# Layer 1's experts as whole fp32 products on column tiles, over 96 or 64 tokens each

## The chip, the cores and the metric

One core of a Trainium2 chip runs the whole program. The metric is device time in microseconds (us), the median of the runs of a kernel. The core has five engines that work side by side: TensorE (PE: matmuls; PEld: its weight loads), VectorE (DVE), ScalarE (ACT), GpSimd (POOL) and SyncE (SP), which issues the large loads from HBM. A matmul takes a stationary operand of up to 128 rows by 128 columns and streams a moving operand of up to 512 columns past it into PSUM, which has 8 banks of 128 rows by 512 fp32 columns.

## The reference

Four layers over 256 tokens of width 1024: two of a first block (a mixed attention layer with a dense feed-forward, then a convolution layer with eight experts), two of a second block (each with cross attention and sixteen small experts). The change is in the eight experts of the first block's second layer, "layer 1":

```
logits = tokens @ router_w                    # 256 tokens, 8 experts
top_vals, top_idx = top_k(logits, 2)          # two experts per token
gates = softmax(top_vals)
y[expert e, its tokens] = (silu(x @ w1[e]) * (x @ w3[e])) @ w2[e]      # 1024 -> 2816 -> 1024, fp32
out[token] = sum over its two experts of gate * y
```

The weights of one expert are three matrices of 1024 x 2816 fp32, 33 MB (of 1,048,576 bytes); eight experts take 264 MB. On the reference's inputs its router sends 79, 56, 13, 76, 83, 72, 64 and 69 tokens to experts 0 to 7.

## The kernel before

**Loads.** All weights come through `raw` (line 193): the next slot of a ring of 8 KB-per-partition slots is taken, and SP issues one load of 1 MB into it. SP works through its loads in program order; a load waits until the last reader of its slot is done. In the experts of layer 1 the ring has 8 slots. Five more slots (`WH1`) belong to `wsplit`.

**fp32 accuracy from fp32r.** `wsplit` (line 243) turns each half of a load into a high part (ScalarE, line 254, a copy to fp32r) and a low part (VectorE, line 255, the difference). `mm3` (lines 187 to 191) then makes three fp32r products: high by high, high by low, low by high.

**An expert of layer 1** (`moe`, class `Job`, line 1201 on). The tokens of an expert are gathered into 128 places by products with a one-hot matrix (line 1191), once for the high and once for the low part of x. `up` (line 1217) goes over the hidden units in blocks of 512 (the last 256): for w1, then for w3, eight 128-row steps of `mm3` with the tokens as stationary operand, then Silu on ScalarE (line 1228) or the product on VectorE (line 1230). `turn` (line 1232) transposes the block's result and splits it, `down` (line 1241) multiplies it by w2 with `mm3` into two banks that hold the expert's output; `combine` (line 1257) splits that, multiplies by the transposed one-hot matrix (line 1265) and adds to the sum with the gate (line 1269). The order in which the parts are written is up(w3) of a block, up(w1) of the next with `turn` inside it, `combine` of the expert before, `down`. A planner places instructions on the engines by its own estimate of their costs, with this order as priority, so that short pieces move between longer ones.

An expert with more than 128 tokens leads to a second pass over all experts, behind a branch (line 1311); no expert of these inputs has so many. Four loads of the next stage (`PRIME`) are issued ahead of the branch.

**The second block's experts** (`moe2`) already work without split weights: 64 gathered tokens per batch, products in fp32 with `tile_position`, that is with the 128 columns of TensorE taken as two tiles of 64, line 1654 (up) and line 1680 (down); the number of an expert can be read from memory into a register of SP (line 1702), and the address of a load follows from it. Other places use four column tiles of 32: adaLN (line 444, 512 columns), the convolution (line 1003, 256 columns), the router (line 1131).

Of the kernel before, what the change touches and what calls it, by code (L numbers as in the profile page):

```python
# [35 lines left out]
MID = 4  # L36
NSLOT, NSLOTB, WHB = 11, 2, 4
CONV = "pvpvpvpp"
PBIG = 8

# [27 lines left out]
def host_consts():  # L68
# [24 lines left out]
    # what a difference has to be above: below zero where the earlier of two equals comes first  # L93
# [61 lines left out]
class Net:  # L155
# [6 lines left out]
    # ---------------------------------------------------------------- helpers  # L162
# [60 lines left out]
    def more_raw(self, name, n):  # L223
        """n more slots for the weights as they come."""
# [6 lines left out]
    def halves(self, name, n):  # L231
        """n slots where wsplit puts its parts."""
# [4 lines left out]
    def take(self, shape, dt, name, p=None):  # L237
        """a tile in a slot of the ring (p, or the one that is free first), until it is given back."""
# [4 lines left out]
    def wsplit(self, x):  # L243
        """raw [128, a, b] -> a pairs (hi, lo) of [128, b]."""
# [14 lines left out]
    def table(self, func):  # L259
        """has ScalarE load the table of func ahead of its use."""  # L260
# [9 lines left out]
    def ordered(self):  # L270
        """a part whose instructions VectorE and ScalarE take in the order given here."""
# [3 lines left out]
    def after(self, *ins):  # L275
        """what follows queues up behind these on their engines."""
# [5 lines left out]
    def rsqrt(self, v, tile=None):  # L282
        """1 / sqrt(v) by Newton's iteration, column by column for the few columns of a tile of its own."""
# [24 lines left out]
    def rms_rstd(self, x2, n, eps, meanwhile=None):  # L308
        """x2: list of lists of APs per token tile, rstd [128, tiles]; meanwhile: what VectorE does before."""
# [19 lines left out]
    def transpose4(self, srcs, name="tp", tag="b"):  # L329
        """up to four [128,128] f32 blocks transposed into one bank."""  # L330
# [5 lines left out]
    def to_T(self, x, hi, lo, cols=slice(0, 256), scale=None, shift=None, k0=0, keep=None):  # L336
        """x: [128, 2, n*128] natural -> hi/lo[:, k0+k, cols]; optional per-feature scale and shift."""
# [21 lines left out]
    def weights_in(self, w, c0, n=512):  # L359
        """w: [1024, *] DRAM view, columns c0..c0+n by 1 MB, as raw() takes them."""  # L360
# [4 lines left out]
    def wstream(self, w, c0, n=512):  # L365
        """(hi, lo) of [128, n] for each 128 rows, in order."""
# [3 lines left out]
    def steps_T(self, w, c0, xT, ntok, evac, n=512, tag="g"):  # L370
        """out[n128, tokens] for each 128 columns; evac(i, psum[:, :ntok]). One step for each 128 rows of w."""
# [14 lines left out]
    def steps_N(self, w, c0, xT, toks, evac, n=512):  # L386
        """out[tok128, n]; evac(i, psum)."""
# [23 lines left out]
    # ---------------------------------------------------------------- setup  # L411
# [62 lines left out]
    def gate_rows(self, mrow, j0, post, dst):  # L474
        """dst[128, 1024] = gt * post_g on every partition."""
# [11 lines left out]
    def norm_T(self, x, hi, lo, cols, sc, pool, tag="raw", bufs=1, fill=0):  # L487
        """modulated rmsnorm of natural x into hi/lo."""
# [8 lines left out]
    def resid(self, y, gp, yg):  # L497
        """X += rmsnorm(y) * gp; y: per token tile two [128,512] APs; yg: room for y * gp, may be y itself."""
# [44 lines left out]
    # ---------------------------------------------------------------- memory keys and values  # L543
# [10 lines left out]
    def last_v(self):  # L554
        """the values of the last layer, from whole operands: no work for ScalarE and VectorE in it."""
# [11 lines left out]
    def fillers(self):  # L567
        """memory keys and values of both layers but for last_v, in steps for where TensorE would wait."""
# [13 lines left out]
    # ---------------------------------------------------------------- layer 0  # L582
    def layer0(self):
# [3 lines left out]
        with ExitStack() as es:  # L587
# [26 lines left out]
            # gates  # L614
# [55 lines left out]
            # lambda  # L670
# [23 lines left out]
            # mLSTM queries, keys, values  # L694
# [34 lines left out]
            # mLSTM: both directions over [x | ctx]  # L729
# [69 lines left out]
            # differential attention  # L799
# [26 lines left out]
            def gate():  # L826
                # output gate of the mLSTM
# [116 lines left out]
    # ---------------------------------------------------------------- layer 1  # L944
# [4 lines left out]
    def conv1(self, mrow):  # L949
        nc, t, tc = self.nc, self.t, self.tc  # L950
        with tc.tile_pool(name="l1", bufs=1) as lp:
# [33 lines left out]
            def conv_pe(i):  # L985
                """four taps at once: 32 channels at each of four shifts on the rows, a column tile for each 32 channels."""
# [104 lines left out]
    def moe_rows(self, mrow, sp):  # L1091
        """rows g*(1+sc) and sh of the second half of layer 1, on every partition."""
# [25 lines left out]
    def logits_in(self, u, uT, tt, copy):  # L1118
        """u [128, 2, 1024], natural, into columns tt of uT [128, KC, 256]."""
# [4 lines left out]
    def logits(self, uT, tt, rw, lt, pl, copy):  # L1124
        """the logits of token tile tt into pl [128, E] of PSUM."""
# [51 lines left out]
    def moe(self, E, F, uh, oh0, G, slot, ci, w1, w3, w2, acc, mp):  # L1177
# [23 lines left out]
        class Job:  # L1201
            """one expert over its gathered tokens, in pieces that the caller interleaves."""
            def __init__(j, w1e, w3e, w2e, oh, gcol, first):
# [6 lines left out]
                if not first:  # L1210
                    j.rest()
# [688 lines left out]
```

## Time and profile before

| | |
|---|---|
| median of 3 runs | 2331.29 us (2331.14 to 2337.98) |
| profiled execution, span from the first to the last instruction | 2325.3 us |
| TensorE / VectorE / ScalarE busy | 2196.3 / 1458.7 / 1115.3 us |
| HBM read | 631.2 MB (10^6 bytes), 272 GB/s over the span |
| share of it for layer 1's experts | 264 loads of 1024 KB |

The profile shows one execution. Busy time counts an engine's own instructions; TensorE's matmuls are pipelined and their ends are modelled, so what it can do is read from the distances between starts and not from busy time. An fp32 matmul leaves two records, an fp32r one leaves one. The idle time before an instruction is put down to what released it.

### The profile page before, as it was taken

The numbers are of one execution on the slowest core, as the hardware profiler recorded it, in microseconds if no ns is written. First come the engines' busy times: TensorE is split into PE (matmuls) and PEld (weight loads), VectorE is DVE, ScalarE is ACT, GpSimd is POOL, SyncE is SP. The second block draws the span as 40 slices with busy tenths as digits, with TensorE's granted clock in tenths as the row PEclk, the third lists the DMA queues.
The fourth block names the chain that finished last, engine by engine and source line by source line (L and its number), as shares of the span: only waits on it lengthen the run. The fifth ranks groups of instructions, "written<-read, shape, count | busy, mean of one in ns | idle before, by whom it ended". The sixth has DMA issues, their size and how long they took to land. (4 is left out here: it accounts for less than half of the span.)

```text
span 2325.3 us, 30656 instructions
## 1 busy us (share of the span) xinstructions
PE 2196.3 (94%) x11817; PEld 1560.6 (67%) x11817; DVE 1458.7 (63%) x2261; ACT 1115.3 (48%) x1530; POOL 82.1 (4%) x121
## 2 busy tenths in 40 slices
PE   6999979999899999999999999988899998999997
PEld 2776648888676888888888888867543436843442
DVE  4464575446886889889898888876622226732223
ACT  3443354335436777777777777765211113421111
POOL 1010100000300000000000000001000001000000
PEclk8999989999999999999999999999899998989998
DMA  7533567863326999999999999966699985499991
GB/s 272 199 110 134 184 228 253 270 223 132 110 92 217 337 343 351 328 344 351 337 354 337 335 335 344 340 231 225 227 392 396 377 306 184 164 365 395 391 364 37
DMA packets 283841, 634.45 MB, mean 273 GB/s; under 512 B 11696, under 2 KB 69168, under 8 KB 277536
## 3 DMA queue, kind: packets, MB, share of 16 engines
q1 hardware_dynamic: 281312, 630.75, 75.5%
q8 instruction: 99, 1.62, 0.3%
q0 software_dynamic: 2080, 1.04, 0.2%
q10 hardware_dynamic: 288, 0.52, 0.1%
q14 instruction: 62, 0.51, 0.1%
HBM read 631.20 MB, written 1.05 MB: 272 GB/s over the span
## 5 line engine op out<-in xcount | busy, mean ns | idle before, releaser
L255 DVE TENSOR_TENSOR wh<-raw,wh 128x1024 fp32r<-128x1024 f32 x710 | 851.8, 1222 | 250.2 <-ACT wh L254 243.9
L254 ACT ACTIVATE wh<-raw 128x1024 fp32r<-128x1024 f32 x710 | 740.5, 1058 | 374.2 <-PE y L191 90.9
L189 PE MATMUL up<-wh,xgh 128*128 128x512 f32 (+1 forms) x768 | 293.2, 382 | 0.0
L190 PE MATMUL up<-wh,xgh 128*128 128x512 f32 (+1 forms) x768 | 289.4, 377 | 0.0
L191 PE MATMUL up<-wh,xgl 128*128 128x512 f32 (+1 forms) x768 | 289.2, 377 | 0.0
L1654 PE MATMUL up<-raw,xg 128*64 128x512 f32 x1088 | 260.2, 596 | 0.0
L1654 PEld LDWEIGHTS up<-raw,xg 128*64 128x64 f32 x1088 | 82.7, 137 | 144.7 <-issue 139.6
L190 PE MATMUL y<-wh,hTh 128*128 128x512 f32 x440 | 173.4, 394 | 0.0
L191 PE MATMUL y<-wh,hTl 128*128 128x512 f32 x440 | 170.1, 396 | 3.4 <-DVE hTl L1238 3.4
L189 PE MATMUL y<-wh,hTh 128*128 128x512 f32 x440 | 171.3, 396 | 0.5 <-ACT hTh L1237 0.5
L191 PEld LDWEIGHTS up<-wh,xgl 128*128 128x128 f32 x768 | 144.3, 188 | 29.1 <-DVE xgl L1197 0.2
L190 PEld LDWEIGHTS up<-wh,xgh 128*128 128x128 f32 x768 | 144.4, 188 | 27.8 <-DVE wh L255 0.2
L189 PEld LDWEIGHTS up<-wh,xgh 128*128 128x128 f32 x768 | 144.3, 188 | 27.8
L1680 PE MATMUL y<-raw,hT 128*64 128x512 f32 x544 | 152.1, 597 | 0.0
L1659 DVE TENSOR_TENSOR h<-up,h 64x512 f32<-64x512 f32 x34 | 23.4, 689 | 199.6 <-ACT h L1658 199.6
L1658 ACT ACTIVATE h<-up 64x512 f32<-64x512 f32 x34 | 20.1, 592 | 198.8 <-PE up L1654 198.8
L1680 PEld LDWEIGHTS y<-raw,hT 128*64 128x64 f32 x544 | 49.1, 136 | 85.1 <-issue 81.7
L189 PE MATMUL gT<-fuTh,wh 128*128 128x256 f32 x352 | 101.0, 287 | 0.0
L190 PE MATMUL gT<-fuTl,wh 128*128 128x256 f32 x352 | 99.5, 283 | 0.0
L191 PE MATMUL gT<-fuTh,wh 128*128 128x256 f32 x352 | 99.5, 283 | 0.0
L191 PEld LDWEIGHTS y<-wh,hTl 128*128 128x128 f32 x440 | 81.9, 187 | 25.5 <-DVE hTl L1238 6.9
L189 PEld LDWEIGHTS y<-wh,hTh 128*128 128x128 f32 x440 | 82.5, 188 | 19.9 <-ACT hTh L1237 0.7
(555 smaller groups left out, 3538.8 us busy)
## 6 DMA issues: line engine op xcount, KB each, us to landing
raw<-in_l_moe_w SPq DMA_DIRECT2D x264, 1024.0 KB, 5.5
raw<-in_w_gate SPq DMA_DIRECT2D x64, 1024.0 KB, 10.5
raw<-in_w_up SPq DMA_DIRECT2D x64, 1024.0 KB, 11.0
raw<-in_w_down SPq DMA_DIRECT2D x64, 1024.0 KB, 9.1
raw<-in_l_mod_w SPq DMA_DIRECT2D x48, 1024.0 KB, 6.3
raw<-in_l_ffn_w SPq DMA_DIRECT2D x33, 1024.0 KB, 5.3
raw<-in_l_w_in SPq DMA_DIRECT2D x14, 1024.0 KB, 5.4
raw<-in_l_conv_pw_w SPq DMA_DIRECT2D x12, 1024.0 KB, 5.6
```

The lines of the kernel that those rows point to most:

```text
L189: mm(out, l[0], r[0], start=start, stop=False, skip_group_check=True)
L190: mm(out, l[0], r[1], start=False, stop=False, skip_group_check=True)
L191: mm(out, l[1], r[0], start=False, stop=stop, skip_group_check=True)
L254: nc.scalar.activation(hi, x[:, k:k + s, :], AF.Copy)
L255: nc.vector.tensor_tensor(lo, x[:, k:k + s, :], hi.bitcast(F32), OP.subtract)
L1654: nc.tensor.matmul(p[o:o + 64, :], xg[:, k, c0:c0 + 64], x[w][:, k - k4, :], start=(k == 0), stop=(k == KC - 1), tile_position=(0, o))
L1658: nc.scalar.activation(h[c0:c0 + 64], p[c0:c0 + 64, :], AF.Silu)
L1659: nc.vector.tensor_tensor(h[c0:c0 + 64], p[o:o + 64, :], h[c0:c0 + 64], OP.mult)
L1680: nc.tensor.matmul(y[o][i * 64:(i + 1) * 64, :], hT[:, q * m + i * 64:q * m + (i + 1) * 64], x[i % len(x)][:, k, o * 512:(o + 1) * 512], s ...
```

## The change

It replaces the products of layer 1's experts. No weight is split; a product is one fp32 matmul. Experts are sorted by their number of tokens (expert 0 is always first, and static, the others are read as register values by SP); the first five (`NL`) get 96 places, the other three 64. `PLACES` is the order in which they run: by places 96, 64, 96, 96, 64, 96, 96, 64. With 96 tokens the columns are four tiles of 32, and the three tiles of tokens by w1 and w3 by two halves of a block make twelve products per 128-row step in three banks; with 64 tokens two tiles of 64 and four products in two banks. Blocks have 1024 hidden units (the last 768), and a load holds two 128-row steps of 1024 columns (4 KB runs; w2: two whole rows per partition, 8 KB runs). Gathered x and the hidden units are kept in fp32; high and low part of x are summed in one bank by the gather. The five slots of `wsplit` join the ring of loads. `combine` has to add two partial results for the second half of the columns when there are 96 tokens. PSUM is divided anew for this stage: three banks for up, two for y, three for the rest. The branch to the second pass is taken when an expert has more tokens than its places. Comments are dropped in the whole file.

```
-MID = 4
+NL, PLACES = 5, (0, 5, 1, 2, 6, 3, 4, 7)
...
     def __init__(j, ws, oh, m, gcol, first):
         ...
+        for k0 in (0, 4):
+            p = self.bank("xg")
+            for i in range(4):
+                o = p[:, i * m:(i + 1) * m]
+                for q in range(4):
+                    nc.tensor.matmul(o, uh[q // 2][:, q % 2, (k0 + i) * 128:(k0 + i + 1) * 128], oh[:, q % 2, :m],
+                                     start=(q == 0), stop=(q == 3))
+            (nc.vector.tensor_copy if k0 else nc.scalar.copy)(xg[:, k0:k0 + 4, :m], ...)
...
     def up(j, i):
+        f0, n = blocks[i]
+        hn, m = n // 2, j.m
+        nb = 3 if m == 96 else 2
+        ps = [self.bank("up", "g") for _ in range(nb)]
+        if m == 96:
+            t, plan = 32, [(0, 0, 0, 0, 0), (0, 1, 0, 0, 32), (0, 2, 0, 0, 64), (0, 3, 0, 1, 64),
+                           (1, 0, 0, 1, 0), (1, 1, 0, 1, 32), (1, 2, 1, 1, 0), (1, 3, 1, 1, 32),
+                           (2, 0, 1, 0, 0), (2, 1, 1, 0, 32), (2, 2, 1, 0, 64), (2, 3, 1, 1, 64)]
+        else:
+            t, plan = 64, [(0, 0, 0, 0, 0), (0, 1, 1, 0, 0), (1, 0, 0, 1, 0), (1, 1, 1, 1, 0)]
+        for k2 in range(0, KC, 2):
+            x = [self.raw(w[:, k2:k2 + 2, f0:f0 + n], 2, n) for w in j.w]
+            for k in range(k2, k2 + 2):
+                for b, c, w, half, s in plan:
+                    nc.tensor.matmul(ps[b][c * t:(c + 1) * t, :hn], j.xg[:, k, s:s + t],
+                                     x[w][:, k - k2, half * hn:(half + 1) * hn], start=(k == 0), stop=(k == KC - 1),
+                                     tile_position=(0, c * t), skip_group_check=True)
+        (three parts of Silu on ScalarE, then three of the product on VectorE; two each with 64 tokens)
...
     def turn(j, i):
+        hv = h[:, :n].rearrange("s (p k) -> s k p", k=nk)      # columns nk apart
+        (nk transposes in groups of four, one copy to SBUF for each group)
...
     def down(j, i):
+        if m == 96:
+            t, one = 32, [(0, 0, 0, 0), (0, 1, 0, 32), (0, 2, 0, 64), (0, 3, 1, 64)]
+            plans = one + [(1, 0, 1, 0), (1, 1, 1, 32)], [(1, 2, 1, 0), (1, 3, 1, 32)] + one
+        else:
+            t, plans = 64, ([(0, 0, 0, 0), (0, 1, 1, 0)],) * 2
+        v = j.w2[f0:f0 + n, :].rearrange("(p k) d -> p k d", k=nk)
+        for k2 in range(0, nk, 2):
+            x = self.raw(v[:, k2:k2 + 2, :], 2, D)
+            for k in range(k2, k2 + 2):
+                for b, c, o, s in plans[k % 2]:
+                    nc.tensor.matmul(j.y[b][c * t:(c + 1) * t, :], hT[:, k, s:s + t],
+                                     x[:, k - k2, o * 512:(o + 1) * 512], ..., tile_position=(0, c * t))
...
     def combine(j):
+            if o and m == 96:
+                nc.scalar.copy(src[:64], y[1][64:128])
+                nc.scalar.copy(src[64:96], y[0][96:128])
+                nc.vector.tensor_tensor(src[:64], y[1][:64], src[:64], OP.add)
...
+    def job(q):
+        if q == 0:
+            return first
+        e = nc.values_load(idx[0:1, q:q + 1], engines=(mybir.EngineType.SP,), min_val=0, max_val=E - 1)
+        m = 96 if q < NL else 64
+        return Job((w1[e], w3[e], w2[e]), onehot(W[:, 0:2, q], m), m, lambda tt: W[:, 2 + tt, q:q + 1], False)
+    units = [(q, i) for q in PLACES for i in range(nb)]
+    for u, (q, i) in enumerate(units):
+        if u == 0:
+            jobs[q] = job(q)
+        jobs[q].up(i)
+        if i == nb - 1 and u + 1 < len(units):
+            q2 = units[u + 1][0]
+            jobs[q2] = job(q2)
+        if i == 1 and behind is not None:
+            jobs.pop(behind).combine()
+            behind = None
+        if u:
+            q1, i1 = units[u - 1]
+            jobs[q1].down(i1)
+            if i1 == nb - 1:
+                behind = q1
+        jobs[q].turn(i)
...
 def moe_layer1(self, gpf):
-    self.ring.extend(extra)
+    self.ring.extend((*extra, *self.wring))
+    self.wring = deque()
+    key = mp.tile([128, 1, E], F32, name="key")         # counts; expert 0 set to 1000
+    place = self.rank(key, self.cst("tie8"), mp, "rp")[:, 0, :]
...
 def run(self):
+    self.banks = {"g": 3, "y": 2, "b": 3}
+    self.psp = e0.enter_context(tc.tile_pool(name="ps2", bufs=1, space=PSUM))
     if "l1" in part:
         self.moe_layer1(gpf)
+    e0.close()
+    self.banks = {"g": 4, "b": 4}
+    self.psp = pool("ps3", space=PSUM)
```

## Rows read from the trace of the kernel before

**Rows 1.** Page: busy tenths of TensorE in 40 equal slices of the span.

```profile
PE   6999979999899999999999999988899998999997
```

**Rows 2.** Windows: us, busy PE, PEld, DVE, ACT, POOL; PEclk, DMA share, GB/s.

```profile
1744.90:1755.20 10.30, 10.30 (x47) 3.34 (x45) 1.18 (x4) 0.73 (x2) 0.00 (x0) 1.00 1.03 405
...
1712.00:1812.00 100.00, 98.75 (x438) 41.34 (x434) 26.48 (x48) 17.48 (x30) 0.00 (x0) 1.00 1.04 394
750.50:1556.50 806.00, 802.42 (x3837) 657.62 (x3835) 710.21 (x687) 604.97 (x655) 0.00 (x0) 1.00 0.95 338
```

**Rows 3.** Waits of SP's queue, 700 to 1560: us in total, times, longest.

```profile
SPq L199 <- DVE wh L255: 668.1, 253, 6.1
```

**Rows 4.** Timeline of layer 1's experts: start, us, engine, line, operation.

```profile
843.33 0.39 PE L189 MATMUL y<-wh,hTh 128*128 128x512 f32 x1
...
847.29 0.40 PE L191 MATMUL y<-wh,hTl 128*128 128x512 f32 x1
...
1545.03 0.60 PE L333 MATMUL hT<-cst,h 128*128 128x128 f32 x4
```

**Rows 5.** Lines by shape, 750.5 to 1556.5: busy us, mean ns, idle before.

```profile
L255 DVE TENSOR_TENSOR wh<-raw,wh 128x1024 fp32r<-128x1024 f32 x522 | 622.6, 1221 | 67.6 <-ACT wh L254 62.5
L254 ACT ACTIVATE wh<-raw 128x1024 fp32r<-128x1024 f32 x523 | 544.7, 1058 | 136.9 <-PE up L191 90.0 <-PE y L191 45.9 <-DVE wh L255 0.7
...
L1230 DVE TENSOR_TENSOR h<-up,h 128x512 f32<-128x512 f32 x40 | 27.4, 686 | 22.6 <-PE up L191 22.6
L333 PE MATMUL hT<-cst,h 128*128 128x128 f32 x174 | 26.6, 272 | 0.0
L1228 ACT ACTIVATE h<-up 128x512 f32<-128x512 f32 x40 | 24.0, 599 | 17.9 <-PE up L191 17.9
...
L1197 DVE CAST xgl<-xg 128x512 fp32r<-128x512 f32 x16 | 10.9, 685 | 0.8 <-PE xg L1191 0.8
```

**Rows 6.** Timeline of TensorE in the second block's experts, 64-column tiles.

```profile
1745.03 0.14 PEld L1654 LDWEIGHTS up<-raw,xg 128*64 128x64 f32 x2 [0.29 <-issue]
...
1751.47 0.14 PEld L1654 LDWEIGHTS up<-raw,xg 128*64 128x64 f32 x1 [0.29 <-issue]
...
1752.42 0.33 PE L1669 MATMUL hT<-cst,h 128*128 128x128 f32 x1
...
1752.68 3.65 PE L1654 MATMUL up<-raw,xg 128*64 128x512 f32 x16
```

**Rows 7.** Timeline of TensorE where it works in 32-column tiles.

```profile
451.73 1.07 PE L444 MATMUL mod<-raw,cs 128*32 128x512 f32 x8
...
604.18 1.07 PE L1003 MATMUL dw<-shs,wd 128*32 128x256 f32 x16
```

**Rows 8.** Window of the gather line L1191 alone: columns PE and PEld.

```profile
750.50:1556.50 806.00, 29.07 (x243) 29.61 (x241) 1.00 0.95 338
```

**Rows 9.** Timelines at the start and the end of layer 1's experts.

```profile
728.15 28.38 SPq L199 DMA_DIRECT2D raw<-in_l_moe_w  x9
...
749.75 1.00 PE L1191 MATMUL xg<-oh,muhl 128*128 128x128 f32 x7 [0.88 <-DVE muhl L1141]
750.59 0.45 PE L189 MATMUL up<-wh,xgh 128*128 128x512 f32 x1
...
753.58 1.16 PE L1191 MATMUL xg<-oh,muhh 128*128 128x128 f32 x6
754.58 1.06 PE L1191 MATMUL xg<-oh,muhl 128*128 128x128 f32 x8
...
1564.14 0.73 PE L1265 MATMUL comb<-yl,oht 128*128 128x512 f32 x2 [1.16 <-DVE yl L265]
1564.68 1.41 DVE L1269 SCALAR_TENSOR_TENSOR macc<-comb,G,macc 128x512 f32<-128x512 f32 x2 [0.59 <-PE comb L1265]
```

**Rows 10.** Timeline of SP's loads between two experts of the second block.

```profile
2106.51 6.29 SPq L199 DMA_DIRECT2D raw<-in_w_down  x4
2113.63 0.37 SPq L199 DMA_DIRECT2D raw<-in_w_gate  x1
```

More of the change, by code (lines that the diff above doesn't have):

```diff
@@ L1232, in turn @@
             def turn(j, i):
-                n = blocks[i][1]
+                n, m = blocks[i][1], j.m
+                nk = n // 128
                 h = j.h.pop(i)
-                pt = self.transpose4([h[:, q * 128:(q + 1) * 128] for q in range(n // 128)], "hT")
-                hT = [mp.tile([128, 512], F32R, tag="hT" + c, name="hT" + c, bufs=2) for c in "hl"]
-                nc.scalar.activation(hT[0][:, :n], pt[:, :n], AF.Copy)
-                nc.vector.tensor_tensor(hT[1][:, :n], pt[:, :n], hT[0][:, :n].bitcast(F32), OP.subtract)
@@ L1239, in turn @@
-                j.hT = hT
+                hv = h[:, :n].rearrange("s (p k) -> s k p", k=nk)
+                j.hT[i] = hT = mp.tile([128, 8, 96], F32, tag="hT", name="hT", bufs=2)
+                for q0 in range(0, nk, 4):
+                    nq = min(4, nk - q0)
+                    p = self.bank("hT")
+                    for q in range(nq):
+                        nc.tensor.transpose(p[:, q * m:(q + 1) * m], hv[:m, q0 + q, :], self.ident[:m, :m])
+                    (nc.vector.tensor_copy if q0 else nc.scalar.copy)(hT[:, q0:q0 + nq, :m],
+                                                                     p[:, :nq * m].rearrange("p (k t) -> p k t", k=nq))
@@ L1257, in combine @@
-            def combine(j):
-                for q in range(2):
-                    y = [self.wkp.tile([128, 512], F32R, tag="room", name="y" + c, bufs=2) for c in "hl"]
-                    self.split(y[0], y[1], j.y[q])
+                    j.y = [self.bank("y", "y") for _ in range(2 if m == 96 else 1)]
+                if m == 96:
+                    t, one = 32, [(0, 0, 0, 0), (0, 1, 0, 32), (0, 2, 0, 64), (0, 3, 1, 64)]
+                    plans = one + [(1, 0, 1, 0), (1, 1, 1, 32)], [(1, 2, 1, 0), (1, 3, 1, 32)] + one
+                else:
+                    t, plans = 64, ([(0, 0, 0, 0), (0, 1, 1, 0)],) * 2
@@ L1270, in combine @@
                                                            op0=OP.mult, op1=OP.add)
-        def transposed(ohf):
-            p = self.bank("ohT")
-            for tt in range(2):
-                nc.tensor.transpose(p[:, tt * 128:(tt + 1) * 128], ohf[:, tt, :], self.ident)
-            o = mp.tile([128, 256], F32R, tag="oht", name="oht", bufs=2)
-            nc.scalar.activation(o, p[:, :256], AF.Copy)
-            return o
-        def job(e):
-            return Job(w1[e], w3[e], w2[e], onehot(iota, slot[:, :, e]) if e else oh0, lambda tt: G[:, tt, e:e + 1], e == 0)
@@ L1283, in moe @@
-        nb = len(blocks)
-        units = [(e, i) for e in range(E) for i in range(nb)]
-        jobs = {0: job(0)}
-        jobs[0].up(0, 0)
-        for q, (e, i) in enumerate(units):
-            jobs[e].up(i, 1)
-            if i == max(0, nb - 2) and e + 1 < E:
-                jobs[e + 1] = job(e + 1)
-            if q + 1 < len(units):
-                e2, i2 = units[q + 1]
-                jobs[e2].up(i2, 0, lambda: jobs[e].turn(i))
-            else:
-                jobs[e].turn(i)
-            if i == 0 and e:
-                jobs.pop(e - 1).combine()
-            jobs[e].down(i)
@@ L1299, in moe @@
-        jobs.pop(E - 1).combine()
+        nb = len(blocks)
+        first = Job((w1[0], w3[0], w2[0]), oh0, 96, lambda tt: G[:, tt, 0:1], True)
+        G = gates()
+        V = mp.tile([128, 4, E], F32, name="V")
+        nc.vector.tensor_copy(V[:, 0:2, :], slot)
+        nc.vector.tensor_copy(V[:, 2:4, :], G)
+        eid = self.cst("eid")[:, :E]
+        is_at = mp.tile([128, E, E], F32, name="is_at")
+        nc.vector.tensor_tensor(is_at, rank[:, None, :].to_broadcast([128, E, E]), eid[:, :, None].to_broadcast([128, E, E]),
+                                OP.is_equal)
@@ new lines, in moe @@
+        q, i = units[-1]
+        jobs[q].down(i)
+        jobs.pop(q).combine()
+        capv = mp.tile([128, E], F32, name="capv")
+        nc.vector.tensor_scalar(capv, rank, float(NL), 32.0, op0=OP.is_lt, op1=OP.mult)
+        nc.vector.tensor_scalar(capv, capv, 64.0, None, op0=OP.add)
+        over = mp.tile([128, E], F32, name="over")
+        nc.vector.tensor_tensor(over, self.count, capv, OP.subtract)
+        ov = mp.tile([128, 1], F32, name="ov")
+        ovi = mp.tile([128, 1], I32, name="ovi")
@@ L1310, in moe @@
-        iota2 = self.cst("iota2")
-        with self.aside(), tc.If(cnt > self.CAP):
+        cnt = nc.values_load(ovi[0:1, 0:1], min_val=0, max_val=256)
+        with self.aside(), tc.If(cnt > self.OV):
+            rp = mp.tile([128, 2, E], F32, name="rp")
+            nc.vector.tensor_tensor(rp, slot, capv[:, None, :].to_broadcast([128, 2, E]), OP.subtract)
             with tc.For_i(0, E, 1) as ei:
@@ L1376, in moe_layer1 @@
         self.ring.extend((self.u1p, *self.memp))
-        self.ring.extend(self.wring)
     def ln_rows(self, gname, bname, gb):
```

188 lines of the change are left out of this document (97 added, 91 removed).

## The prediction

> **What bounds the kernel now.** I read the slices of the span first [rows 1]: from the 14th to the 26th the digits of TensorE stand at 9 without a break. That is the expert stage of layer 1, from the first gather of expert 0 to the last product. A table of its stretch [rows 2] gives TensorE busy 802.4 of 806.0 us at the full granted clock (1.00), VectorE 710, ScalarE 605, and 338 GB/s; the stretch 1712 to 1812, in the experts of the second block, gives 394 GB/s with the same queue. So the stage does not take weights as fast as they can come. The DMA queue's own waits [rows 3] say why: 668 us for the vector split of a weight tile, that is for a slot to be given back, and the split in turn follows TensorE (ScalarE's high parts wait 90 us for it [rows 5]). Single matmuls then [rows 4]: from 843.33 to 847.29 eighteen passes of 512 columns start 0.233 us apart without a gap. The stage is bound by the number of fp32r passes: 484 matmuls per expert, 100.8 us (806/8) per expert.
>
> **What the change removes.** All three-pass products on split weights go, with the ScalarE and VectorE splits (544.7 and 622.6 us) [rows 5]. The splits alone bound nothing, since TensorE hid them; what counts is TensorE's own list.
>
> **What it puts there.** One fp32 product of 512 columns leaves two records. In the second block a pair of them on 64-column tiles starts every 0.43 us per record: 15 steps from 1745.03 to 1751.47 make 0.4293 us [rows 6]. So a slot, in which all column tiles work at once, is 2 x 0.4293 = 0.859 us. Do four 32-column tiles share one slot as two 64-column tiles do? [Rows 7]: the adaLN product puts four 512-column products (x8) in 1.07 us; the convolution puts two fours of 256 columns, with new weights for each, (x16) in 1.07 us. One after the other the first would need 3.4 us. They share it.
>
> Count the slots. With 96 tokens a 128-row step has 12 products of 32 tokens, three slots; 16 such steps at 512 columns (two blocks of 1024 hidden units) and 8 at 384 (the block of 768, three quarters of a slot) make 16 x 3 + 8 x 3 x 0.75 = 66; down, 22 steps of 6 products, 33. Together 99 slots, 85.0 us. With 64 tokens it is 16 x 2 + 8 x 2 x 0.75 + 22 = 66 slots, 56.7 us. The router of the reference sends 79, 56, 13, 76, 83, 72, 64, 69 tokens to the eight experts: experts 0, 4, 3, 5, 7 fall to the 96 places and 6, 1, 2 to the 64 ones, and nobody has more tokens than places (expert 6 has 64 of 64). 5 x 99 + 3 x 66 = 693 slots, **595 us**.
>
> What stays on TensorE, at the spacing of the rows: gathers 29.1 us [rows 8]; 176 transposes of hidden units, 26.6 us busy with the tail of each group [rows 5], of which a group of four lasting 0.60 with 0.27 for each (1545.03) [rows 4] shows 0.11 to be the spacing, 19; combining 64 products at their 0.233 [rows 4], 15; one-hot transposes 2: **65 us**. That the transposes now read every sixth or eighth column shows in no row: between nothing and 0.43 - 0.11 each (a whole 512-column record in place of a transpose), 0 to 56 us; I take nothing, since the row nearest to it is the transpose itself.
>
> New are the changes between column tiles and the whole array. A lone transpose between up products starts at 1752.42 and the up products go on at 1752.68 [rows 6]: 0.26 where 0.11 would do, and the transpose itself came 0.1 late, 0.25 us for a round trip. I count 12 per expert (six transpose groups, gather halves, one-hot, combining by halves): 96 x 0.25 = **24 us**; bounds 10 (the order puts them together) and 40.
>
> Waits. (a) The first up product now needs the whole gather, high and low parts summed in one bank, where before it started at 750.59 with half the high part. The low part is there at 749.75; the halves of the gather that came later cost 1.16 and 1.06 us, the copy 0.69 [rows 5, 9]: first up at about 754.0. (b) The first unit has no down product to hide its evacuation: Silu 0.60 and product 0.69 on 512 columns, three of each in two engines, 3 us. Later units have 7 to 13 us of down there, so they pay nothing; the three banks of an up product are free again by then. (c) Combining: in the kernel before, TensorE waits 1.16 us for the second half of the low part (1564.14) [rows 9], and the change puts two copies and a sum ahead of that half; 2 us per expert, 16 us. If the planner lifts these ahead, 0; if it puts them behind the next Silu, 6 each, 48. (d) The new VectorE work (order of the experts, sorted slots, gates) is some 15 operations of 0.2 to 0.4 us, needed by the second expert, 85 us later: nothing. If it lands ahead of the first gather's copy, 1 to 4. (e) SP reads the expert number for seven experts. Behind the waiting read stand only weight loads; in the second block, where the same read stands between two experts, the queue goes on 0.83 us after the last load of the one (2106.51 + 6.29 to 2113.63) [rows 10], against a ring that grows from 8 to 13 slots (the five split slots join it), 13 x 2.6 = 34 us of loads: nothing.
>
> Sum for TensorE: first up at 754.0, then 595 + 65 - 3.6 (the first gather lies before) + 24 + 3 + 16 = 699, to 1453; the last combining ends 5 later, 1458. Before, the last accumulation ended at 1566.1 (1564.68 + 1.41). Gain **108 us**.
>
> Now the other resource. 264 loads of 1 MB (the last blocks: 0.75 MB, more of them; the bytes are the same), two landed before 728, where the slots open [rows 9]. The 4 KB-run loads of the second block run at 405 GB/s, mixed ones at 394 [rows 2]: 2.59 to 2.66 us per load, 262 loads 679 to 697 us, from about 731 to 1410..1428, and some 12 us of work behind the last: 1422 to 1440. So the loads are 18 to 36 us ahead of TensorE at the end: close, and a 96-token expert needs more of TensorE (85 + 8 + 5 = 98) than of the queue (33 x 2.62 = 86), a 64-token one less (70). During one of the latter the ring loses (86 - 70)/2.62 = 6 of its 13 loads and gains 4 or 5 back in each of the former; in the order 96, 64, 96, 96, 64, 96, 96, 64 it does not run dry. TensorE stays the bound.
>
> What follows the stage (residual, second block) keeps its instructions; the four primed loads find free slots as before, and it moves up as a whole.
>
> The profiled execution spans 2325.3 us, the median of the runs is 2331.29; the 6.0 us between lie outside the span and stay. 2331.3 - 108 = **2223 us**.
>
> On the packing, a rule speaks against this sum. The Trainium skill ("TensorE: Matmul & The Clock Gate", Measured speedup vs the span model) gives 2.38 for three column tiles, not 3. A slot of four would by that share take 0.859/0.79 = 1.08 us, an estimate from that page. The trace disagrees at 256 columns with two fours in a row [rows 7]; at 512 columns only single fours are seen.
>
> **Rivals.**
> 1. The loads set the pace: the planner hides switches and waits, TensorE is at 754 + 595 + 61 = 1410, and the stage ends at 1422 to 1440, a gain of 126 to 144: about 2197. For it: the two are within 5%. Against it: [rows 6] shows the switch cost paid even where TensorE had time.
> 2. More is lost at hand-overs: three units per expert, each 2 us late for banks or transposes, 48 us more (or the strided transposes at their upper bound): 2271. For it: only two y banks and three up banks, each with one user at a time. Against it: the down product between.
> 3. Fours don't pack when they follow each other. If each of the 5 x 99 = 495 carries the 0.21 us by which the single four [rows 7] exceeds 0.859, that is 104 us and the gain is gone: about 2327, and the rule above, with 0.22, would give 2332. If they go two and two, 495 x 0.859 = 425 us: **2648, slower**. It decides from 1.08 us per four on (0.859 + 108/495). Against it: the 16 records of the convolution, where the second four follows at once.
> 4. The change doesn't do what it says: one token more on expert 6 and the second pass runs, eight experts by three batches of 33 loads: 792 x 2.62 = 2075 us more. The reference's count is exactly 64.
>
> **Chances.** Forecast as summed (2200 to 2250) 0.57; rival 1 0.14; rival 2 0.17; rival 3 0.05 with the gain gone, 0.05 slower; rival 4 0.02. A measurement of this kernel tells about 0.3% (7 us) from no change. Faster: 0.57 + 0.14 + 0.17 + 0.02 (half of the rival 3 that loses part) = 0.90; same 0.02; slower 0.08. The range takes in rivals 1 and 2 and leaves out 3 and 4 with the far ends of 1 and 2: 2182 to 2276.
>
> **What would show it.** In the trace after, fours of up records 0.43 us apart, four starting together; 99 slots make one 96-token expert 95 to 100 us from its first up to the next, a 64-token one 68 to 73; VectorE and ScalarE under 20% busy in the stage; 370 to 395 GB/s; SP waiting for TensorE (up, y), not for VectorE. Rival 1: TensorE waiting for loads in most experts. Rival 2: TensorE idle at transposes and combining, over 6 us per expert. Wrong altogether: steps over 0.5 us within a four, a lower granted clock in the stage, or a stage end outside 1420 to 1510.

## The result, and the profile after

The changed kernel takes 2257.19 us (median of 4 runs, 2250.77 to 2258.73); the kernel before took 2333.53 us in the same comparison. The ratio is 0.9665, 95% interval 0.9646 to 0.9684: faster by 76 us. The forecast was 2223 us and 108 us, so the direction and the bound were right, and 32 us of the gain are missing (38 us between the two profiled spans, 2325.3 and 2255.5 us, a gain of 69.8).

Page of the changed kernel, TensorE's busy tenths in 40 slices (answers to [rows 1]): 9 without a break from the 15th slice to the 26th. The stage now begins in the 14th (768.8 of 56.4 us each), where the 8 is, and ends in the 27th, where the 7 is.

```profile
PE   5999888999999899999999999979899998899996
```

Window of the stage, first up product to last accumulation (columns as in [rows 2]):

```profile
768.77:1496.50 727.73, 718.62 (x5519) 269.00 (x5518) 94.31 (x154) 67.11 (x128) 0.00 (x0) 1.00 0.96 370
```

TensorE is busy 98.7% at the full clock, VectorE 13% and ScalarE 9% (before 88% and 75%), and 370 GB/s come in where it was 338. SP's waits (columns as in [rows 3]) are now for TensorE in the main; the vector split, 668 us before, is left with 6.6:

```profile
SPq L199 <- PE up L1225: 363.6, 148, 7.2
SPq L199 <- PE y L1271: 173.9, 79, 6.2
```

So the stage is still TensorE's. But busy time can't say whether its slots are full. A whole block does what was forecast: 192 records of up, eight in a slot, are 24 slots, 20.6 us at 0.859, with the transposes ahead of them and down behind without a gap (timeline of the changed kernel, columns as in [rows 6]):

```profile
1030.94 1.05 PE L1250 MATMUL hT<-cst,h 96*128 96x96 f32 x6
1031.91 20.85 PE L1225 MATMUL up<-raw,xg 128*32 128x512 f32 x192
1052.54 2.80 PE L1271 MATMUL y<-raw,hT 128*32 128x512 f32 x24
```

Elsewhere single gather products (xg) or pairs of combining products stand between the up products:

```profile
1004.01 0.31 PE L1198 MATMUL xg<-oh,muhl 128*128 128x96 f32 x1
1004.15 0.27 PE L1198 MATMUL xg<-oh,muhh 128*128 128x96 f32 x1
1004.36 2.77 PE L1225 MATMUL up<-raw,xg 128*32 128x384 f32 x28
1007.06 0.31 PE L1198 MATMUL xg<-oh,muhh 128*128 128x96 f32 x1
1007.30 2.13 PE L1225 MATMUL up<-raw,xg 128*32 128x384 f32 x20
1009.37 0.42 PE L1198 MATMUL xg<-oh,muhl 128*128 128x96 f32 x2
```

Between them stand 28 and 20 records, that is 14 and 10 products, no multiples of four. My own reading of the starts of the records shows what that does: the last two products of such a run find no partner and have a slot for themselves.

```
1007.30  4 steps with four tiles each (8 products), 0.329 us a step
1008.62  1 step with two tiles,                     0.322 us
1008.94  1 step with two tiles (2 products),        0.423 us, then the gather
```

The start of the stage looks different too. Timeline of the changed kernel (answers to the first lines of [rows 9]), and the window of the same stretch in the changed kernel:

```profile
740.70 3.65 PE L333 MATMUL tp<-cst,macc 128*128 128x128 f32 x16 [6.94 <-DVE macc L1074]
...
748.84 3.75 PE L561 MATMUL lv<-raw,memF 128*128 128x512 f32 x4 [0.50 <-PE logit L1134]
...
752.57 12.52 PE L561 MATMUL lv<-raw,memF 128*128 128x512 f32 x28
764.53 0.72 PE L1198 MATMUL xg<-oh,muhh 128*128 128x96 f32 x2
...
768.77 0.64 PE L1225 MATMUL up<-raw,xg 128*32 128x512 f32 x4
```

```profile
733.40:752.50 19.10, 10.88 (x61) 6.91 (x60) 13.75 (x52) 8.36 (x18) 0.00 (x0) 0.57 0.82 320
```

and in the kernel before, where the 32 products of the last memory values (L561) filled the same wait for the residual:

```profile
728.20 8.75 PE L561 MATMUL lv<-raw,memF 128*128 128x512 f32 x20
...
742.64 3.68 PE L561 MATMUL lv<-raw,memF 128*128 128x512 f32 x8
```

```profile
733.00:752.50 19.50, 17.58 (x101) 10.36 (x100) 17.77 (x61) 12.13 (x23) 0.00 (x0) 0.96 0.90 330
```

They come after the router now, and TensorE, idle for 7 us, has a granted clock of 0.57 over the stretch in place of 0.96. The change opens the new banks of the expert stage ahead of these products; as I read the code, those come free only when the residual has read the old ones (the first experiment moves the opening). From the last product of the convolution stage to the first up product it takes 35.4 us (733.36 to 768.77); 26.0 were forecast (727.96 to 754.0).

What follows the stage is unchanged: from the last accumulation to the end of the span 759.0 us, before 759.2 ([rows 9]: 1564.68 + 1.41). The timeline's last accumulation:

```profile
1495.10 1.41 DVE L1299 SCALAR_TENSOR_TENSOR macc<-comb,W,macc 128x512 f32<-128x512 f32 x2 [0.89 <-PE comb L1295]
```

So the 38 us between the two spans are 9.4 us of late start, 23.7 us inside the stage (727.7 for 699 + 5) and 5.4 us in identical work ahead of the stage, less 0.2 behind it. The 5.4 us are no part of the change: over all traces here the last product of the convolution stage starts between 728.0 and 738.4 us. The prediction took the 6.0 us between the span and the median for time outside the span; in every execution with both on record that time is 1.7 to 1.9 us (2257.27 and 2255.5 here), so the kernel before was profiled in an execution some 4 us shorter than its median. The medians, which leave this out, miss 32 us.

This table splits the stage between the first up product and the last combining product, for the changed kernel and for two of the experiments below. It is my own sum over the starts of TensorE's records: a nominal 0.4293 us for each half of a slot (three quarters of it at 384 columns), 0.112 for a gather product or transpose, 0.233 for a combining product; what a step takes beyond that is put to the kind of step. A wait of 0.7 us at the first product of a combining stands with the changes (three of them in the changed kernel, one each in the others). Of the 6.7 us of waits in the changed kernel 2.6 are at combining; the rest is ahead of transposes in the three experts of 64 places, and none of it in the first unit, for which the forecast had 3 us:

```profile
PE hT L1250 <- DVE h L1237: 3.5, 3, 1.2
```

| us | forecast | changed | b_order | c_mid |
|---|---|---|---|---|
| products, slots full | 595 | 595.0 | 595.0 | 595.0 |
| half-filled slots | 0 | 26.6 | 0 | 0 |
| product steps beyond the nominal | 0 | 6.6 | 16.2 | 5.8 |
| gathers, transposes, combining | 61.4 | 61.1 | 61.1 | 61.1 |
| beyond the nominal inside their groups | 0 | 7.3 | 6.1 | 5.5 |
| changes to the whole array and back (number) | 24 (96) | 22.8 (98) | 9.8 (39) | 9.0 (39) |
| waits ahead of transposes and at combining | 19 | 6.7 | 24.7 | 4.3 |
| sum | 699 | 726.1 | 712.8 | 680.8 |

### The profile page after: what moved, and what is told of

It reads as the page before. It is cut to its first block, busy times and chain, and to the rows that moved or that the text cites. A ratio compares the mean times of both kernels' runs of the same rounds, so it can differ in the third digit from the quotient of the medians.

```text
span 2255.5 us, 32795 instructions
## 1 busy us (share of the span) xinstructions
PE 2115.4 (94%) x13497; PEld 1175.0 (52%) x13497; DVE 834.8 (37%) x1739; ACT 571.1 (25%) x995; POOL 79.4 (4%) x121
## 3 DMA queue, kind: packets, MB, share of 16 engines
HBM read 631.20 MB, written 1.05 MB: 280 GB/s over the span
## 5 line engine op out<-in xcount | busy, mean ns | idle before, releaser
L1225 PE MATMUL up<-raw,xg 128*32 128x512 f32 (+3 forms) x3456 | 437.6, 559 | 0.1
L255 DVE TENSOR_TENSOR wh<-raw,wh 128x1024 fp32r<-128x1024 f32 x182 | 222.0, 1226 | 180.4 <-ACT wh L254 179.3
L1225 PEld LDWEIGHTS up<-raw,xg 128*32 128x32 f32 (+1 forms) x3456 | 147.5, 114 | 250.8 <-issue 237.4
L254 ACT ACTIVATE wh<-raw 128x1024 fp32r<-128x1024 f32 x182 | 190.6, 1058 | 232.1 <-PE gT L191 89.0
L1271 PE MATMUL y<-raw,hT 128*32 128x512 f32 (+1 forms) x1584 | 215.7, 597 | 0.0
L1237 DVE TENSOR_TENSOR h<-up,h 64x512 f32<-64x512 f32 (+5 forms) x63 | 40.8, 648 | 387.4 <-ACT h L1235 386.7
L1271 PEld LDWEIGHTS y<-raw,hT 128*32 128x32 f32 (+1 forms) x1584 | 60.4, 115 | 121.4 <-issue 114.3
L444 PE MATMUL mod<-raw,cs 128*32 128x512 f32 x384 | 62.7, 684 | 29.9 <-DMA raw<-in_l_mod_w 29.9
L1767 DVE TENSOR_TENSOR X<-comb,X 128x512 f32<-128x512 f32 x72 | 47.0, 687 | 72.3 <-PE comb L1766 72.2
L189 PEld LDWEIGHTS gT<-fuTh,wh 128*128 128x128 f32 x352 | 67.4, 191 | 12.1 <-issue 10.9
L191 PEld LDWEIGHTS gT<-fuTh,wh 128*128 128x128 f32 x352 | 67.5, 192 | 0.3
L190 PEld LDWEIGHTS gT<-fuTl,wh 128*128 128x128 f32 x352 | 67.4, 192 | 0.2
## 6 DMA issues: line engine op xcount, KB each, us to landing
raw<-in_w_gate SPq DMA_DIRECT2D x64, 1024.0 KB, 10.7
```

The lines of the kernel that those rows point to most:

```text
L189: mm(out, l[0], r[0], start=start, stop=False, skip_group_check=True)
L190: mm(out, l[0], r[1], start=False, stop=False, skip_group_check=True)
L191: mm(out, l[1], r[0], start=False, stop=stop, skip_group_check=True)
L254: nc.scalar.activation(hi, x[:, k:k + s, :], AF.Copy)
L255: nc.vector.tensor_tensor(lo, x[:, k:k + s, :], hi.bitcast(F32), OP.subtract)
L444: nc.tensor.matmul(p[32 * j:32 * j + 32, :], self.cs[:, k, :], x[:, 0, j * 512:(j + 1) * 512], start=(k == 0), stop=(k == KC - 1), tile_po ...
```

## The experiments

Medians, each of 4 runs; the ratio is to the kernel before, with its 95% interval. The intervals are about 4 us wide to either side, so two kernels a few us apart are told apart by their traces and not by the medians.

| | us | ratio | interval |
|---|---|---|---|
| changed kernel | 2257.2 | 0.9665 | 0.9646 to 0.9684 |
| a_banks | 2249.4 | 0.9635 | 0.9617 to 0.9653 |
| b_order | 2241.5 | 0.9612 | 0.9596 to 0.9628 |
| ab_both | 2232.2 | 0.9572 | 0.9556 to 0.9588 |
| c_mid | 2202.3 | 0.9430 | 0.9401 to 0.9460 |
| c_ring8 | 2227.5 | 0.9550 | 0.9521 to 0.9579 |
| c_sorted | 2231.6 | 0.9567 | 0.9538 to 0.9596 |
| c_512 | 2219.2 | 0.9508 | 0.9477 to 0.9538 |
| c_96 | 2286.7 | 0.9799 | 0.9783 to 0.9816 |
| c_64 | 2177.0 | 0.9327 | 0.9312 to 0.9343 |
| after_ring8 | 2261.4 | 0.9697 | 0.9679 to 0.9714 |

**a_banks: the banks switched behind the memory values.**

```
 def run(self):
-            e0.close()
-            self.banks = {"g": 3, "y": 2, "b": 3}
-            self.psp = e0.enter_context(tc.tile_pool(name="ps2", bufs=1, space=PSUM))
+            (the same three lines as a function, self.switch)
...
 def moe_layer1(self, gpf):
             self.last_v()
+            self.switch()
```

> Undoes one part of the change: the set of PSUM banks is switched behind the last product of memory values (the 32 products of L561), not ahead of it, so the order of instructions may put these products into TensorE's wait for the residual again, as in the kernel before. Theory 1 (the late start comes from them): in the changed kernel the gather of expert 0 starts at 764.5 though its low parts are there at 756.3, and the router's small products (740.7 to 752.5) run 2.5 us longer than before at a lower granted clock; both go, and the time falls by 8 to 11 us, to about 2247. Theory 2 (the gather waits for something else that is as late, or the products take the clock or the slots elsewhere): within 3 us of 2257.

Measured 2249.4, 7.8 us less: just under the 8 to 11 of theory 1, and outside the 3 us of theory 2. The products of L561 start right behind the convolution stage again, and the window of the router has its clock back:

```profile
733.40:752.50 19.10, 17.63 (x100) 9.54 (x99) 17.98 (x78) 10.49 (x21) 0.00 (x0) 1.00 0.92 348
```

The first up product comes 24.9 us behind the last product of the convolution stage in place of 35.4. The 24.9 us still hold a wait of the gather, 1.4 us for a copy of L564. Of the 10.5 us won, 2.5 are lost at once: the first six steps of the up products take 0.85 us in place of 0.43.

**b_order: TensorE in the written order.**

```
+with tc.manual_schedule(engines={mybir.EngineType.PE}):
     (the loop over units as in the changed kernel, moved in)
```

> The changed kernel, but TensorE takes the instructions of the expert stage in the order in which the program writes them (all products of an up block, then the gather or the combining, then the down block, then the transposes), not in the order of the planner, which puts single gather products and pairs of combining products between them. In the changed kernel TensorE changes 98 times from column tiles to the whole array, and 77 slots by my count hold two products in place of four. Theory 1 (half-filled slots and changes cost the time): the half-filled slots go (77 x 0.43 = 33 us) and about 57 of the 98 changes at 0.29 us (16 us); the combining written as a block waits for its second half, up to 2.4 us for each expert as at the end of the stage (17 us): 2208 to 2240, about 2225. Theory 2 (the insertions filled waits for weights): TensorE waits for loads where the insertions stood, and the time stays at 2250 to 2265.

Measured 2241.5, 15.7 us less: between the two ranges, 1.5 us above that of theory 1 and 8.5 us below that of theory 2. The table above settles which: the half-filled slots are gone to the last one, the changes fell from 98 to 39, and the list of waits names none for weights in their place (theory 2 falls). What ate the gain is the combining, and more than the 17 us allowed for it. Waits of TensorE in this kernel, and one combining of it:

```profile
PE comb L1295 <- DVE yl L1291: 14.8, 9, 2.5
PE comb L1295 <- ACT yh L1290: 4.8, 9, 0.7
```

```profile
976.12 0.50 PE L1295 MATMUL comb<-yh,oht 64*128 64x512 f32 x1 [0.45 <-ACT yh L1290]
979.09 0.79 PE L1295 MATMUL comb<-yl,oht 64*128 64x512 f32 x1 [2.47 <-DVE yl L1291]
979.68 0.62 PE L1295 MATMUL comb<-yh,oht 64*128 64x512 f32 x1
980.11 0.62 PE L1295 MATMUL comb<-yl,oht 64*128 64x512 f32 x1
980.66 11.71 PE L1271 MATMUL y<-raw,hT 128*32 128x512 f32 x84
```

The second half waits for its high and low parts: 22.0 us over 16 waits, by the starts. Both halves use the same two tiles, and the high part (yh) of the second half starts when the products of the first have read theirs. The longer wait is for the low part (yl), which stands on VectorE behind three products of the up block (L1237) and the accumulation of the first half (L1299):

```profile
974.76 2.10 DVE L1237 TENSOR_TENSOR h<-up,h 64x512 f32<-64x512 f32 x3 [20.20 <-ACT h L1235]
975.47 0.59 ACT L1290 ACTIVATE yh<-y 64x512 fp32r<-64x512 f32 x1 [0.74 <-PE comb L1295]
976.90 1.41 DVE L1299 SCALAR_TENSOR_TENSOR macc<-comb,W,macc 128x512 f32<-128x512 f32 x2
978.34 0.69 DVE L1291 TENSOR_TENSOR yl<-y,yh 64x512 fp32r<-64x512 f32 x1
```

And the wait is paid a second time: the products behind it take 0.62 us where 0.39 is usual, and the down slots that follow start 0.85 us apart before they return to 0.43. Over the stage 38 product steps over the nominal by more than 0.1 us make 14.5 us, which neither theory expected. Not all of it is behind a wait: 10.7 us follow the combining of six of the eight experts, but 3.0 us follow two gathers, at 838 and 1187 us, in which TensorE waited for nothing. The windows of the first gather and of the down products behind it show the granted clock fall from 1.00 to 0.50:

```profile
838.00:841.80 3.80, 3.80 (x36) 3.68 (x34) 1.73 (x4) 0.65 (x2) 0.00 (x0) 1.00 1.02 411
842.40:845.40 3.00, 3.00 (x20) 0.74 (x16) 0.15 (x1) 0.00 (x0) 0.00 (x0) 0.50 1.03 414
```

**ab_both: the two edits together.**

> Both edits: the banks switched behind the memory values, and TensorE's order as written in the stage. Theory 1 (TensorE's own list is the bound, the two costs are apart from each other): the two gains add, about 2214 (2197 to 2232). Theory 2 (loads are the next bound): 262 loads at 2.62 us from 722 end at 1408, and with the work behind the last one the stage can't end before about 1420, so the gain over the changed kernel can't pass 75 us (2182); if the ring of 13 slots runs dry in the experts of 64 places, the sum of the two gains isn't reached and TensorE shows waits for raw of 3 us and more in each of these experts.

Measured 2232.2, 25.0 us less, against 7.8 + 15.7 = 23.5 for the two alone: they add, within the noise, and the sum lands at the upper end of theory 1 (2197 to 2232), short by the combining; its list of waits names none for weights, which theory 2 would need. Windows behind one of its combining waits show what the slow steps are:

```profile
970.50:974.40 3.90, 3.90 (x25) 1.03 (x28) 1.06 (x2) 0.00 (x0) 0.00 (x0) 0.56 1.05 408
974.40:982.20 7.80, 7.80 (x80) 2.32 (x72) 0.00 (x0) 0.00 (x0) 0.00 (x0) 1.00 1.01 406
```

The granted clock behind the wait is 0.56, near the lower of its two levels (1.2 of 2.4 GHz), and then 1.00. The Trainium skill ("TensorE: Matmul & The Clock Gate", HAM oscillation — how this bites in real kernels) tells of a kernel in which waits for loads make TensorE fall back to the lower clock, so that the matmuls behind each wait start slowly; these two rows agree, behind a wait for VectorE. The gathers above show the same fall without a wait.

**c_mid: both edits, and the combining without waits.**

```
-yg = [self.wkp.tile(..., tag="room", bufs=2) for c in "hl"]
+yg = [mp.tile(..., tag="y" + c) if o else self.wkp.tile(..., tag="room", bufs=2) for c in "hl"]
 def up(j, i, mid=None):
     for k2 in range(0, KC, 2):
+        if k2 == 4 and mid:
+            mid()                   # combine of the expert before
```

> Built on the kernel with both edits (banks switched late, TensorE in written order). There, TensorE stands 1.4 us twice at each combining of an expert (16 waits, 22.0 us together) because both halves share two tiles for their high and low parts, and behind each wait some 4 us of products run at twice the spacing (0.85 us for 0.43), 41 steps, 14.5 us over the nominal. Now the second half has two tiles of its own and the combining stands in the middle of the up block, behind its fourth 128-row step, when its operands have been ready for long. Theory 1 (wait and clock): 19 us of the waits (the last expert keeps its own) and 11 of the slow steps go: 2232 - 30, about 2202 (2194 to 2210). Theory 2 (the loads are the next bound): the ring runs dry in the experts of 64 places, TensorE waits for raw there, and less than half of it is seen: 2214 to 2230.

Measured 2202.3 us (runs from 2197.9 to 2208.1): theory 1. One combining of this kernel takes 2.2 us (960.00 to 962.24) where it took 6.2 (974.47 to 980.66), with no wait in it; the clock over the stage is 0.99 (b_order 0.97), the loads come at 396 GB/s:

```profile
763.23:1446.00 682.77, 676.04 (x5519) 252.23 (x5518) 93.05 (x154) 67.01 (x128) 0.00 (x0) 0.99 1.00 396
```

Which of the two edits does it, the place or the tiles, was not tried apart. The last combining has tiles of its own too, but nothing to stand in the middle of, and there TensorE still waits 1.5 us for the low part of the second half:

```profile
1443.40 0.50 PE L1298 MATMUL comb<-yl,oht 64*128 64x512 f32 x1 [1.53 <-DVE yl L1294]
```

This version beats both kernels, by 129 us (ratio 0.943, 0.940 to 0.946) and by 55 us. From first up to first up, behind the first expert (89.9), its experts of 96 places take 92.6 to 95.0 us and those of 64 places 69.3.

**c_ring8, c_sorted, c_512: how much of this hangs on the loads.** Five slots fewer in the ring; `PLACES = (0, 1, 2, 3, 4, 5, 6, 7)`; w1 and w3 by 512 columns.

> The kernel with the combining in the middle of the up block, but the five slots of the split weights don't join the ring: 8 slots in place of 13. The loads now land 2.5 us apart when nothing holds them. An expert of 64 places is 66 slots of 0.859 and some 9 us of other work, 66 us, for 33 loads that take 82, so it falls 16 us behind. Theory 1 (the lead of the ring is what hides this): 8 slots, of which two or three are in use, hold 12 to 15 us; 2 to 5 us are lost in each of three experts, and 96-place experts lose nothing: 5 to 15 us more than c_mid. Theory 2 (the lead doesn't matter, TensorE is far from the loads): within 3 us of c_mid.

> The kernel with the combining in the middle of the up block, the experts in the order of their tokens: all five of 96 places, then the three of 64. Theory 1 (an expert of 64 places lives on the lead of the ring): three in a row fall 48 us behind, the ring of 13 covers 25 to 30; 15 to 25 us more than c_mid, with TensorE waiting for raw in the last two experts. Theory 2 (the order doesn't matter): within 3 us.

> The kernel with the combining in the middle of the up block, but w1 and w3 loaded as in the kernel before, by 512 columns of four 128-row steps (runs of 2 KB, 1.5 KB in the last block) in place of 1024 columns of two. In the kernel before such loads landed 2.7 us apart, those of 4 KB runs 2.56. 22 of the 33 loads of an expert are of this kind. Theory 1 (TensorE is the bound and the ring covers it): an expert of 64 places falls 4 us further behind; 0 to 8 us more than c_mid. Theory 2 (the loads set the pace): 8 x 22 x 0.2 = 35 us more loads show, 20 to 35 us.

Measured 25.3, 29.3 and 16.9 us more than c_mid. In the first two the lead of the ring matters, by more than theory 1 had it; in the third both theories miss, theory 1 by 9 us and theory 2 by 3. Waits of TensorE for weights, of which c_mid's list has none; c_ring8:

```profile
PE up L1227 <- DMA raw<-in_l_moe_w: 10.3, 11, 1.1
PE y L1273 <- DMA raw<-in_l_moe_w: 5.1, 10, 0.7
```

c_sorted, and a window in its last two experts, TensorE 87% busy and the loads at their limit:

```profile
PE up L1227 <- DMA raw<-in_l_moe_w: 16.4, 15, 1.7
PE y L1273 <- DMA raw<-in_l_moe_w: 4.8, 10, 0.6
```

```profile
1300.00:1450.00 150.00, 129.89 (x610) 49.27 (x608) 18.22 (x30) 11.65 (x23) 0.00 (x0) 1.00 1.02 412
```

c_512 (and 0.7 us for down):

```profile
PE up L1229 <- DMA raw<-in_l_moe_w: 8.7, 8, 2.3
```

The waits alone are 15 of the 25, 21 of the 29 and 9 of the 17 us. Some of the rest is half-filled slots again: by the starts 42 steps in c_ring8, 42 in c_512 and 64 in c_sorted hold fewer products than they have tiles, and none in c_mid. As I read it, a wait in the middle of a step cuts it. The balance is not accounted for in full.

**after_ring8: the same question of the changed kernel itself.** 8 slots in the ring, nothing else.

> The changed kernel itself, with 8 slots in the ring in place of 13 (the five slots of the split weights stay out). Theory 1 (in the changed kernel TensorE's half-filled slots make it so slow that the loads, 33 x 2.5 = 82 us for each expert, are hardly behind it: an expert of 64 places takes it 77 us from first up to first up, one of 96 over 100): 0 to 5 us more than the changed kernel, 2257 to 2262. Theory 2 (the lead of the ring is spent there as it is where TensorE's order is as written, where 8 slots cost 25 us): 2272 to 2285.

Measured 2261.4, 4.2 us more, about as much as the medians scatter: theory 1. There TensorE's slower list hides what the ring is for.

**c_96 and c_64: all experts of one kind.** `NL = 8`; all jobs with m = 64, which leaves the tokens beyond the 64th of five experts out of the result: c_64 is a measurement and no version of the kernel.

> The kernel with the combining in the middle of the up block, but all eight experts at 96 places. Theory 1 (TensorE's slots are the bound, 99 for one against 66): 3 x 33 x 0.859 = 85 us more, 2280 to 2295. Theory 2 (the experts of 64 places already run at the pace of the loads, 82 us each, against some 93 for one of 96): 3 x 11 = 33 us more, 2230 to 2245.

> The same with all eight experts at 64 places: tokens beyond the 64th of five experts are left out of the result, and the pass for what is over isn't taken. TensorE has 8 x 66 slots and some 9 us more for each, 526 us. Theory 1 (the loads land 2.5 us apart where nothing holds them): 264 loads from 722 on, the last at 1382, the stage ends near 1400 where it ended near 1436: some 36 us less than c_mid, 2160 to 2175. Theory 2 (2.59 to 2.66, the rate of the second block on which the prediction rests): the last load at 1410 to 1428, the stage end at 1425 to 1443, 2190 to 2210. In both TensorE waits for raw throughout.

c_96 measured 2286.7, 84.4 us more for 85 expected: 33 slots of 0.859 for each of three experts, theory 1, and nothing of the pace of the loads. c_64 measured 2177.0, 25.3 us less, between the two theories, 2 us from the range of theory 1 and 13 from that of theory 2. The rate was not what either used: 412 GB/s over 800 to 1400, 2.55 us for 1.05 MB, but the first 80 us bring less, since the slots come free late:

```profile
720.00:760.00 40.00, 38.52 (x183) 24.47 (x184) 24.23 (x95) 15.19 (x33) 0.00 (x0) 0.93 0.78 286
760.00:800.00 40.00, 38.55 (x187) 13.90 (x185) 3.62 (x6) 3.11 (x6) 0.00 (x0) 0.98 0.93 370
800.00:1400.00 600.00, 525.98 (x2482) 210.88 (x2480) 68.46 (x119) 45.67 (x93) 0.00 (x0) 0.99 1.02 412
```

From the first up product to the last accumulation c_64 takes 659 us (757.6 to 1417.0), bound by the loads, with 75 us of waits for them; c_mid takes 682 (763.2 to 1445.4), bound by TensorE and with the same bytes. The two limits are 3% apart.

## Why the prediction was right in kind and 32 us short

- **The slot of four.** Right. Fours follow each other at 0.859 us, and the 693 slots counted from the code take 595.0 us in b_order and c_mid. Rival 3 falls, and with it, for fours that follow each other, the share that the Trainium skill gives ("TensorE: Matmul & The Clock Gate", Measured speedup vs the span model, 2.38 of 3): the trace disagrees, four tiles of 32 columns at 512 columns share a slot in full.
- **That all slots would be full: the term that was mis-sized.** "Count the slots" took fours across the whole stage as unbroken. The planner puts short pieces between up and down products, which the description of the kernel says it does, and where it cuts a run that isn't a multiple of four products, two of them take a slot alone. 26.6 us, nothing in the forecast. b_order shows it: the slots alone go to zero with the order. Why the planner cuts there was not tried.
- **The first up product.** Forecast at 26.0 us behind the convolution stage, came at 35.4. The gather's parts were costed rightly (a_banks: 24.9); what was missed is an edit that was read as a division of PSUM only: opening the banks ahead of `last_v` moves 13.7 us of products (32 at 0.43) out from under the residual. Worth 7.8 us by a_banks.
- **Changes between tiles and whole array.** 96 at 0.25 forecast, 98 at 0.23 in the trace. The price was right; that the number came out is luck. The forecast counted 48 of them for transposes, and the trace has 32; the gathers are cut in 40 places and the combining in 26. In the written order there are 39.
- **Waits at combining.** 16 us forecast, 2.6 in the changed kernel by the table (4.3 by its list of waits, which counts the first product of a combining too): the very cuts that spoil the fours hide them. Written in one block they cost 22.0 and the clock behind them 10.7 more (b_order), inside the bound of 48.
- **The strided stationary operand of the transposes.** Taken as nothing, bounded at 56 us. The weight load of a transpose takes 211 ns on average where it took 140, but by my reading of the starts the transposes of a group follow each other in 0.112 us as before; nothing was right.
- **The loads.** "TensorE stays the bound" and "the ring does not run dry" hold in the changed kernel (its list of waits in the stage names none for weights). The ring's lead, counted as needed, is needed only once TensorE keeps its slots full (25.3 us in c_ring8, 4.2 in after_ring8).
- **Rival 2** had 2271, nearer in time than the forecast, but by TensorE idle at transposes and combining, over 6 us for each expert. The trace has 6.7 us of such waits in the whole stage: its time came near by another mechanism.
- **The signs named.** Fours 0.43 apart, VectorE and ScalarE under 20%, 370 GB/s, SP waiting for up and y: all seen. Experts of 95 to 100 and 68 to 73 us: 99.8 to 102.6 and 76.5 to 77.3 in the changed kernel, 92.6 to 95.0 and 69.3 in c_mid; the first expert, with no down product or combining of another in it, takes 86.0 and 89.9. The stage's end, 1496.5, lies where the forecast allowed it, but late.

With the two misses taken out and the combining moved, the kernel is at 2202, below the 2223 of the forecast: the sum had 24 us for changes and 19 for waits, and c_mid spends 9.0 and 4.3. So the forecast was nearer than its terms: these two were too large by 30 us there, and half-filled slots and the late start were missing.

## What to carry to other kernels

When products share a slot in column tiles, count the cuts as well as the products: a short instruction between two of them costs its own time, a change of a quarter us, and half a slot if the run isn't a multiple of the tiles. When memory is divided anew, ask which work was filling a wait across that line. And a wait of TensorE can be paid twice, once as the wait and once at the lower clock behind it, as behind six of the eight combinings of b_order.

## What was not expected of the hardware

The price of a wait behind the wait: in b_order 22.0 us of idle time at combining came with 10.7 us of slow product steps behind it (granted clock 0.56 in such a stretch of ab_both). Nor does it take a wait: behind two gathers of b_order (granted clock 0.50) and one of c_mid, at 1256 us, the products were as slow with TensorE busy throughout, 3.0 and 1.2 us. Against it, the many short waits for weights in c_sorted, 1.7 us the longest, left the clock at 1.00 with TensorE idle 13% of the time (its window above). What decides was not tried. And loads of 4 and 8 KB runs held 412 GB/s over 600 us, above the 405 on which the forecast rested.
